# A hybrid SSM and gated-delta layer on one core: where the recurrence's buffers lie, who loads its tables, and what stands beside the last norm

## Chip, cores and metric

The kernel runs on one core of a Trainium2 chip. The metric is device time in microseconds of one launch. A core has five engines with an instruction queue each: TensorE (PE; its weight loads are shown as PEld), VectorE (DVE), ScalarE (ACT), GpSimd (POOL) and SyncE (SP), which here only issues DMAs. ACT and POOL can issue DMAs too. An engine takes its instructions in order, so one that waits holds up all behind it.

## What is computed

One layer of a decoder for 1024 prompt tokens and 8 decode rows, in float32, with model width 1024:

- `h = rms_norm(x)`, then one wide projection `h @ w_in` into z, x/B/C, dt, q/k/v, a gate, beta, a, and two merge gates.
- A Mamba-2 branch: causal convolution of width 4, silu, then a chunked scan with a state per head. `S <- S * decay + B^T (dt x)`, and `y = (masked C B^T) (dt x) + C S`; then `y = rms_norm((y + D x) * silu(z))` in four groups of 512 channels.
- A gated delta branch: convolution, silu, l2 norms of q and k, and per chunk and head the solve of a unit lower triangular system `(I + A) sol = rhs`, then the recurrence `v_new = u - w S`, `o = q_g S + (masked q k^T) v_new`, `S <- S * g + k_g^T v_new`; then `rms_norm(o) * silu(gate)`.
- `x += (sigmoid(m1) * (y @ W1) + sigmoid(m2) * (o @ W2)) @ w_out`, then a SwiGLU feed-forward of width 2816, a per-layer embedding gated by a sigmoid, and a final rms_norm.
- The last states of both branches are outputs, for the prompt and, after one step, for the 8 decode rows.

## The kernel before

**Dense work.** A wide product is made of dense tiles of 128 output channels: 8 blocks of input channels times 3 chunks of 344 tokens (1032 tokens in all). Each float32 product is three matmuls of rounded parts (`wh*h`, `wh*l`, `wl*h`, lines 159 to 178), so a dense tile is 72 matmuls. Before each tile its weights are loaded by SP into `wraw`, ACT rounds them into `wh` (L138) and DVE makes the rest `wl` (L139). Results leave PSUM by an ACT copy.

**Order.** The pieces of the program are written as one sequence, and a planner decides at build time, with a model of durations, in which order each engine gets its instructions; only a few stretches have a PE order written out by hand (`weave`, which lays dense tiles between the steps of the scan). The order is fixed at run time. A tile of a pool with a tag and `bufs` buffers takes a buffer that is free by the planner's clock; the instruction that first writes it waits on the chip until the earlier user is done with it.

**The scan.** `ssd(g)` runs the Mamba-2 scan for channel group g (four groups) over 8 chunks. Its result is written in place into four tiles `X[0..3]` (named `Xt`, 1024 columns each, pool `sa`). After the last chunk the state is transposed by PE, copied by ACT into `so` (L923) and written out (L924). `so` has the tag `sdt`, of which there is one buffer; the other users of that buffer are `u` in `ssm_dec` (L750 to 752), the first operation of the decode step, and `vbd` in the decode step of the delta branch. `ssm_dec` loads decode states into tiles of the tag `sd`, of which there are four buffers, updates them on DVE (L753) and writes them out (L754).

**The gate and the norm of a group.** `ssm_gate` multiplies `X` by silu(z) and sums squares into `sqs`; between its steps stand calls of `ssm_dec`. `ssm_norm_out(g)` makes row sums on PE, a square root and a reciprocal, sends the 1024 factors through DRAM (`rn_d`, L957) to get them on all partitions (`srb`, L959), multiplies `X` (L961) and writes it to `y_d` from ACT's queue (L962). For g = 0 to 2 it is called within the next group's convolutions. After the last group two dense tiles are left over of a list of filler tiles (`fill(FILL[4] - 2, FILL[4])`); they stand ahead of `ssm_norm_out(3)`.

**The recurrence of the delta branch.** When the scan's pools close, three pools open in their space: `gr0` (`r0`), `gr2` (`r2`) and `gr1` (`r1`), in this order. The loop at the end runs over 8 chunks with a pair of units each, `unit(0, c)` and `unit(1, c)`, four heads to a unit. A unit

1. loads `at` (256 KB) and, for each of four 32-row blocks, a piece of a table of inverted diagonal blocks into `U` (`EB<-e_d`, L1050, 16 KB) and, for three of them, its transpose into `db` (`DB<-dd_d`, L1052, 16 KB). Between them POOL zeroes the diagonal blocks of `at` (L1053). So a unit has seven table loads, all on SP, ahead of its loads of `kg`, `qg`, `qk` and `vb`;
2. multiplies `at` and `db` on PE, copies the product into `MT` (ACT, L1063), and builds the rest of the inverse in `U` in three steps of PE and DVE (L1071);
3. takes the old state off (`res`, L1080 and L1081, from the second chunk on), multiplies by `U`, copies to `vn` (L1087), makes the new state `gs`, the output `on`, its norm and its transpose, and writes it to `og_d` (L1119) from the same tile `on`.

`EB`, `DB` and `MT` are zeroed once by POOL at the start (L1032), which may only happen when what lay in their space is dead. `MT` is in `r1`; `res` shares the tag `on` (two buffers) with `on`; `gs` (four buffers) and `vn` (two) are in `r2`.

Beside the units of a chunk PE has dense tiles: the filler tiles from 15 on for chunks 0 to 3, the SSM branch product (from `y_d`) for chunks 4 to 6.

If the pools lie as they are declared, the tile sizes in the code put the scan's tiles at (KiB per partition) 0 to 12 solve tables, 12 to 41 `sw`, 41 to 49 `Bt` and `Ct`, 49 to 65 the four `Xt`; and the recurrence's before at 0 to 8 `EB`, 8 to 12 `DB`, 12 to 34 the loads, 34 to 38 `kt`, 38 to 42 `on`, 42 to 46 `vn`, 46 to 54 `gs`, 54 to 58 `MT`. So `MT` and half of `gs` lie where `Xt` was.

Of the kernel before, what the change touches and what calls it, by code (L numbers as in the profile page):

```python
# [8 lines left out]
F32 = mybir.dt.float32  # L9
# [7 lines left out]
P = 128  # L17
# [16 lines left out]
FILL = (3, 6, 9, 12, 15, 17, 20, 22, 24)  # L34
# [5 lines left out]
def hybrid_step(  # L40
# [9 lines left out]
    V, S, G, TE = nc.vector, nc.scalar, nc.gpsimd, nc.tensor  # L50
    dma = nc.sync.dma_start
# [148 lines left out]
    hacts, hs = half_slabs("h")  # L200
# [13 lines left out]
    e_d = dr.tile([8, 4, NC, 32, 32], F32, name="e_d")  # L214
    dd_d = dr.tile([8, 4, NC, 32, 32], F32, name="dd_d")
# [25 lines left out]
    with (  # L241
# [3 lines left out]
        r0 = gain_cols(p0)  # L245
# [205 lines left out]
    def fill(lo, hi):  # L451
        for _ in fill_units(lo, hi):
            pass
# [249 lines left out]
    dp = pD.enter_context(tc.tile_pool(name="dp", bufs=1, reuse_waits="tile"))  # L703
# [70 lines left out]
    with (  # L774
# [63 lines left out]
        def ssd(g, Bt, Ct, X):  # L838
# [80 lines left out]
            t = pt.tile([P, 512], F32, name="pt")  # L919
            for i in range(4):  # L920
                TE.transpose(t[:, i * P : i * P + P], st[:, i * P : i * P + P], ident)
            so = dp.tile([P, 4, P], F32, name="so", tag="sdt")
            S.copy(so.rearrange("p i n -> p (i n)"), t)  # L923
            dma(o_ssm_p[0, 0, h0 : h0 + 8].rearrange("(i a) q n -> (a q) i n", a=2), so)  # L924

# [24 lines left out]
        def ssm_norm_out(g, X, sqs):  # L950
            t = pt.tile([P, 512], F32, name="pt")
            row_sums(t, sqs)
            rr = dp.tile([P, P], F32, name="srr", tag="sdj")
            S.activation(rr, t[:, :P], AF.Sqrt, bias=b_eps, scale=1.0 / 512)
            V.reciprocal(rr, rr)
            for j in range(2):
                dma(rn_d[g, 4 * j : 4 * j + 4], rr[j::32])  # L957
            rb = s1.tile([P, NP], F32, name="srb", tag="sqs")
            dma(rb, rn_d[g].rearrange("c l -> (c l)").partition_broadcast(P))  # L959
            for i in range(4):  # L960
                V.scalar_tensor_tensor(X[i], X[i], gain(G_SSM, 4 * g + i), rb, ALU.mult, ALU.mult)  # L961
                S.dma_start(y_d[4 * g + i], X[i])  # L962

        last, side = None, solves()
        for g in range(4):
# [14 lines left out]

            weave(ssd(g, Bt, Ct, X), 17, units(), 3 * (FILL[g + 1] - FILL[g]) + 6, side)
            last = ssm_gate(g, X, zs)
        fill(FILL[4] - 2, FILL[4])
        ssm_norm_out(3, *last)
        for _ in side:
            pass
        for i in range(28, 32):
# [35 lines left out]
    with (  # L1023
# [3 lines left out]
    ):  # L1027
        EB = [r0.tile([P, 4, P], F32, name=f"EB{i}") for i in range(4)]
        DB = [r0.tile([P, 4, P], F32, name=f"DB{i}") for i in range(2)]
        MT = [r1.tile([P, 4, P], F32, name=f"MT{i}") for i in range(2)]  # L1030
        for t in EB + DB + MT:
            G.memset(t, 0.0)  # L1032
        state = [None, None]
# [4 lines left out]
        def unit(b4, c):  # L1038
            hs = slice(4 * b4, 4 * b4 + 4)
            U, db = EB[(2 * c + b4) % 4], DB[b4]  # L1040
# [6 lines left out]
            at = load(at_d, "at2")  # L1047
            for b in range(4):
                r = slice(32 * b, 32 * b + 32)
                dma(U[r, :, r], e_d[hs, b, c].rearrange("h j i -> j h i"))  # L1050
                if b < 3:
                    dma(db[r, :, r], dd_d[hs, b, c].rearrange("h j i -> j h i"))  # L1052
                G.memset(at[r, :, r], 0.0)  # L1053
            kg, qg, qk, vb = load(ktok_d, "kg"), load(qg_d, "qg2"), load(qk_d, "qk2"), load(vb_d, "vb2")
            kt = r2.tile([P, 4, C], F32, name="kt2")
# [19 lines left out]
            if c > 0:  # L1075
                ks = quad(py.tile([P, 512], F32, name="py"))
                for h in range(4):
                    mm(ks[:, h], kt[:, h], s[:, h])
                r = r2.tile([P, 4, P], F32, name="res", tag="on")
                V.tensor_tensor(r, ks, bc(fkb[:, c, hs], 2, [P, 4, P]), ALU.mult)  # L1080
                V.tensor_tensor(vb, vb, r, ALU.subtract)  # L1081
                yield 1
            vp = quad(py.tile([P, 512], F32, name="py"))
            for h in range(4):
                mm(vp[:, h], U[:, h], vb[:, h])
            vn = r2.tile([P, 4, P], F32, name="vn")
            S.copy(vn, vp)  # L1087
            yield 1
            up = quad(py.tile([P, 512], F32, name="py"))
            for h in range(4):  # L1090
                mm(up[:, h], kg[:, h], vn[:, h])
            s2 = r2.tile([P, 4, P], F32, name="gs", bufs=4)
            if c == 0:
                V.tensor_copy(s2, up)
            else:
# [675 lines left out]
```

## Time and profile before

| | |
|---|---|
| median of 3 runs | 2613.71 us (2613.59 to 2615.52) |
| the profiled execution | 2612.65 us, its span 2610.6 us, mean granted TensorE clock 0.996 |
| PE busy | 2561.8 us, 98% of the span |
| DVE, ACT, POOL busy | 1778.1, 1120.2, 264.0 us |
| DMA | 320 MB, 123 GB/s over the span |

The span runs from the first instruction to the last; 2.05 us of the execution's time lie outside it. PE is busy all but some 49 us. The scan's four groups run from about 425 to 1105 us, the last norm and the start of the recurrence lie at 1107 to 1185 us, and the recurrence ends at about 1535 us. A matmul's busy time overlaps the next one's, so rates are read from counts in a stretch, not from busy times.

### The profile page before, as it was taken

To read this page: it belongs to the slowest core of one execution; us is meant where nothing else is said; L and a number is where in the kernel's file an instruction comes from. 1 tells how busy PE (TensorE), PEld (TensorE's weight loads), DVE (VectorE), ACT (ScalarE), POOL (GpSimd) and SP (SyncE) were. 2 spreads that over 40 slices of the span, in tenths; PEclk is the share of its full clock that TensorE was granted. 3 is DMA by queue.
4 is the path that set the end of the run, shared out by engine and by line. 5 is a ranking of instruction groups with operands and counts; after the bars stand their busy time and mean duration, and the time that the engine had idled before them with its cause. 6 is when DMAs were issued, how large, how long until landed. Compare 5 with 4: busy or idle time off the path is not lost.

```text
span 2610.6 us, 46496 instructions
## 1 busy us (share of the span) xinstructions
PE 2561.8 (98%) x18155; PEld 2484.8 (95%) x18155; DVE 1778.1 (68%) x3328; ACT 1120.2 (43%) x2328; POOL 264.0 (10%) x537
## 2 busy tenths in 40 slices
PE   8999999999999999999999999999999999999998
PEld 7999999989999999889999988999999999999998
DVE  5677786698896775664455566457777777777665
ACT  5456556365373473542342235345222222223344
POOL 0221111121220210300000000012000000000110
PEclk9999999999999999999999999999999999999999
DMA  4354453444443352276664456535111111111222
GB/s 129 117 177 150 146 173 120 116 147 132 136 150 113 126 162 87 86 228 197 181 205 146 123 181 235 164 115 171 50 49 49 55 54 56 49 49 45 62 84 91
DMA packets 429913, 320.16 MB, mean 123 GB/s; under 512 B 43537, under 2 KB 392634, under 8 KB 428414
## 3 DMA queue, kind: packets, MB, share of 16 engines
q1 hardware_dynamic: 425148, 304.19, 38.6%
q10 hardware_dynamic: 2626, 8.97, 0.9%
q0 software_dynamic: 1920, 4.03, 0.4%
q8 instruction: 143, 2.34, 0.4%
q14 instruction: 76, 0.62, 0.1%
HBM read 236.64 MB, written 80.74 MB: 122 GB/s over the span
## 4 chain that ended last, share of the span: by engine, by line
PE 84%; DVE 5%; DMA 5%; ACT 3%; issue 2%; POOL 0%; SPq 0%; DVEq 0%; ACTq 0%; POOLq 0%
PE pd L69 62%; PE py L69 10%; PE pt L69 6%; PE pz L69 3%; DMA out_dram<-so 1%; DVE wl L139 1%; ACT sdt L752 1%; DMA bc<-bcd_d 1%; DVE sdj L758 1%; PE pt L856 0%; DMA eb<-eas_d 0%; DMA sg<-gate_d 0%; DVE ca L574 0%; DMA pe_d<-g 0%; DVE sd L753 0%
## 5 line engine op out<-in xcount | busy, mean ns | idle before, releaser
L69 PE MATMUL pd<-h,wh 128*128 128x344 f32 x4080 | 988.1, 324 | 2.4 <-ACT wh L138 1.7
L69 PEld LDWEIGHTS pd<-h,wh 128*128 128x128 f32 x4080 | 706.0, 189 | 10.5 <-issue 5.1
L69 PE MATMUL pd<-h,wl 128*128 128x344 f32 x2040 | 659.3, 323 | 2.4 <-DVE wl L139 2.2
L138 ACT CAST wh<-wraw 128x512 fp32r<-128x512 f32 (+1 forms) x354 | 216.7, 613 | 520.3 <-PE pd L69 357.4
L69 PEld LDWEIGHTS pd<-h,wl 128*128 128x128 f32 x2040 | 385.5, 189 | 5.3 <-DVE wl L139 4.1
L139 DVE TENSOR_TENSOR wl<-wraw,wh 128x512 fp32r<-128x512 f32 (+1 forms) x354 | 246.8, 698 | 196.0 <-ACT wh L138 190.3
L69 PE MATMUL pd<-gu,wh 128*128 128x344 f32 (+2 forms) x1056 | 248.6, 319 | 0.0
L69 PE MATMUL pd<-y,wh 128*128 128x344 f32 x768 | 187.7, 325 | 0.0
L69 PEld LDWEIGHTS pd<-gu,wh 128*128 128x128 f32 x1056 | 182.4, 188 | 0.0
L69 PE MATMUL pd<-gu,wl 128*128 128x344 f32 (+2 forms) x528 | 169.2, 320 | 0.0
L1566 DVE TENSOR_TENSOR acc<-acc,pd 128x344 f32<-128x344 f32 x216 | 109.6, 511 | 44.0 <-PE pd L69 39.8
L69 PEld LDWEIGHTS pd<-y,wh 128*128 128x128 f32 x768 | 132.7, 189 | 1.8 <-issue 0.8
L69 PE MATMUL pd<-y,wl 128*128 128x344 f32 x384 | 123.8, 322 | 0.0
L560 ACT COPY raw<-pd 128x344 f32<-128x344 f32 x144 | 62.6, 438 | 118.0 <-PE pd L69 108.9
L69 PE MATMUL pd<-bq,wh 128*128 128x258 f32 (+1 forms) x572 | 108.1, 285 | 0.0
L69 PEld LDWEIGHTS pd<-gu,wl 128*128 128x128 f32 x528 | 99.2, 188 | 0.0
L574 DVE SCALAR_TENSOR_TENSOR ca<-raw,cwm,ca 128x1056 f32<-128x1056 f32 x72 | 96.4, 1338 | 2.0
L574 DVE SCALAR_TENSOR_TENSOR ca<-raw,cwg,ca 128x1056 f32<-128x1056 f32 x72 | 95.3, 1323 | 1.5
L849 ACT ACTIVATE ab<-ab,ncolA 128x128 f32<-128x128 f32 x256 | 81.8, 391 | 33.3 <-POOL ab L845 27.2
L69 PE MATMUL pd<-o,wh 128*128 128x344 f32 x384 | 92.3, 323 | 3.0 <-DVE sgp L1351 2.2
L69 PE MATMUL pd<-h,gw 128*128 128x384 f32 (+1 forms) x576 | 94.8, 323 | 0.0
L69 PE MATMUL pd<-mx,wh 128*128 128x258 f32 x512 | 92.8, 283 | 0.0
(584 smaller groups left out, 5221.7 us busy)
## 6 DMA issues: line engine op xcount, KB each, us to landing
wraw<-in_w_in_dram SPq DMA_DIRECT2D x87, 512.0 KB
ab<-acs_d SPq DMA_DIRECT2D x32, 512.0 KB
out_dram<-sd SPq DMA_DIRECT2D x48, 256.0 KB
wraw<-in_w_ffn_in_dram SPq DMA_DIRECT2D x24, 512.0 KB
ru<-in_w_ffn_in_dram SPq DMA_DIRECT2D x22, 512.0 KB
wro<-in_w_ffn_out_dram SPq DMA_DIRECT2D x72, 128.0 KB
sg_d<-mg SPq DMA_DIRECT2D x16, 516.0 KB
bb<-rk_d SPq DMA_DIRECT2D x8, 1024.0 KB
```

The lines of the kernel that those rows point to most:

```text
L69: TE.matmul(o, l, r, start=start, stop=stop)
L138: S.copy(wh[:, :n], raw[:, k0 : k0 + n])
L139: V.tensor_tensor(wl[:, :n], raw[:, k0 : k0 + n], wh[:, :n].bitcast(F32), ALU.subtract)
L560: S.copy(raw[:, 3 + t0 : 3 + t0 + n], o[:, :n])
L574: V.scalar_tensor_tensor(ca, raw[:, j : j + CONVN], w[j], ca, ALU.mult, ALU.add)
L752: S.activation(u[:, b], bcs[0][:, b], AF.Copy, scale=xdtd[:, pair, bb : bb + 1])
L758: V.scalar_tensor_tensor(t, s[:, b], 1.0, bcs[1][:, b], ALU.mult, ALU.mult, accum_out=ydec[g][:, i % 4, bb : bb + 1])
L849: S.activation(ab[:, h], ab[:, h], AF.Exp, bias=ncolA[:, c, h0 + h : h0 + h + 1])
L1566: V.tensor_tensor(a, a, o, ALU.add)
```

## The change

```diff
@@ ssd, after the last chunk
-            so = dp.tile([P, 4, P], F32, name="so", tag="sdt")
+            so = dp.tile([P, 4, P], F32, name="so", tag="sd", bufs=4)
@@ after the last group
-        fill(FILL[4] - 2, FILL[4])
+        fill(FILL[4] - 2, FILL[4] - 1)
         ssm_norm_out(3, *last)
+        fill(FILL[4] - 1, FILL[4])
@@ the recurrence's tiles
-        MT = [r1.tile([P, 4, P], F32, name=f"MT{i}") for i in range(2)]
+        MT = [r0.tile([P, 4, P], F32, name=f"MT{i}") for i in range(2)]
+        GS = [(r0 if i < 3 else r1).tile([P, 4, P], F32, name=f"gs{i}") for i in range(4)]
@@ unit
-                dma(U[r, :, r], e_d[hs, b, c].rearrange("h j i -> j h i"))
+                G.dma_start(U[r, :, r], e_d[hs, b, c].rearrange("h j i -> j h i"))
                 if b < 3:
-                    dma(db[r, :, r], dd_d[hs, b, c].rearrange("h j i -> j h i"))
+                    G.dma_start(db[r, :, r], dd_d[hs, b, c].rearrange("h j i -> j h i"))
                 G.memset(at[r, :, r], 0.0)
@@
-                r = r2.tile([P, 4, P], F32, name="res", tag="on")
+                r = r2.tile([P, 4, P], F32, name="res", bufs=1)
@@
-            vn = r2.tile([P, 4, P], F32, name="vn")
+            vn = r0.tile([P, 4, P], F32, name="vn", bufs=2)
@@
-            s2 = r2.tile([P, 4, P], F32, name="gs", bufs=4)
+            s2 = GS[(2 * c + b4) % 4]
```

There are six edits. The scan's last state goes out through a tile of the tag `sd` instead of `sdt`. One of the two filler tiles is written behind the last norm. `MT`, `vn` and three of the four `gs` are in `r0`, the pool that lies lowest; by the same arithmetic `MT` is then at 12 to 16 KiB, the three `gs` at 16 to 22, the loads at 22 to 44 with `vn` behind them, and only `kk`, `dd`, the fourth `gs` and part of `on` are left where `Xt` was. The states `gs` are four named tiles instead of four buffers in turn. `res` has a buffer of its own. And the 112 table loads (7 for each of 16 units) are issued by POOL instead of SP.

## Rows read from the trace of the kernel before

**Rows 1.** The page's first part: each engine's busy time, share of the span and instructions.

```profile
PE 2561.8 (98%) x18155; PEld 2484.8 (95%) x18155; DVE 1778.1 (68%) x3328; ACT 1120.2 (43%) x2328; POOL 264.0 (10%) x537
```

**Rows 2.** Who PE waited for, over the whole span: who, then us in total, times, longest.

```profile
PE pt L69 <- DMA EB<-e_d: 4.1, 1, 4.1
PE pd L69 <- DVE wl L139: 3.6, 4, 1.2
PE pt L69 <- ACT MT L1063: 2.3, 1, 2.3
PE pd L69 <- ACT wh L138: 1.7, 1, 1.7
PE pt L69 <- issue: 1.3, 1, 1.3
```

**Rows 3.** PE in three stretches: from and to, length, busy us (matmuls), granted clock, DMA share, GB/s.

```profile
571.10:580.70 9.60, 6.90 (x25) 0.64 0.58 171
...
600.00:620.00 20.00, 20.00 (x128) 1.00 0.64 217
...
1143.30:1154.10 10.80, 6.71 (x26) 0.68 0.92 276
```

**Rows 4.** ACT's instructions in order of time at the end of the first scan: start, duration, engine and line; in brackets the idle time ahead and what ended it.

```profile
567.00 1.28 ACT L752 ACTIVATE sdt<-bc,xdtd 128x128 f32<-128x128 f32 x4 [3.71 <-DMA out_dram<-so]
...
572.34 0.62 ACT L138 CAST wh<-wraw 128x512 fp32r<-128x512 f32 x1
```

**Rows 5.** PE's instructions in order of time at the same place.

```profile
571.03 0.32 PE L69 MATMUL pd<-h,wl 128*128 128x344 f32 x1
573.01 0.58 PE L69 MATMUL pd<-h,wh 128*128 128x344 f32 x2 [1.66 <-ACT wh L138]
574.63 0.65 PE L69 MATMUL pd<-h,wl 128*128 128x344 f32 x1 [1.04 <-DVE wl L139]
```

**Rows 6.** SP's DMA issues around the first scan's end: the last two of four loads into `sd`, the write of `so`, the first decode state's write, and the next load into `sd`.

```profile
523.79 1.49 SPq L748 DMA_DIRECT2D sd<-in_state_ssm_dram  x2
...
562.19 0.58 SPq L924 DMA_DIRECT2D out_dram<-so  x1
568.69 0.38 SPq L754 DMA_DIRECT2D out_dram<-sd  x1
572.17 0.38 SPq L748 DMA_DIRECT2D sd<-in_state_ssm_dram  x1
```

**Rows 7.** SP's DMA issues at the recurrence's start, of the second unit of chunk 0: `at`, and the last piece of `DB`; then PE's product of the two in PE's order of time.

```profile
1128.27 1.08 SPq L1044 DMA_DIRECT2D at<-at_d  x1
...
1143.14 0.50 SPq L1052 DMA_DIRECT2D DB<-dd_d  x1
...
1147.53 1.99 PE L69 MATMUL pt<-DB,at 128*128 128x96 f32 x8 [4.09 <-DMA EB<-e_d]
```

**Rows 8.** POOL's instructions in order of time at the recurrence's start.

```profile
1136.56 0.90 POOL L1053 MEMSET at<- 32x128 f32 x4 [24.02 <-DMA at<-at_d]
...
1159.98 0.90 POOL L1053 MEMSET at<- 32x128 f32 x4 [19.44 <-DMA at<-at_d]
1160.93 1.00 POOL L1032 MEMSET MT<- 128x512 f32 x2
```

**Rows 9.** ACT's copies into `MT` for both units of chunk 0, and in the chain of work that ended last (start, us, what) the load of `at` for chunk 1.

```profile
1161.50 0.95 ACT L1063 COPY MT<-pt 128x384 f32<-128x384 f32 x2 [5.24 <-POOL MT L1032]
...
1150.83 9.04 DMA at<-at_d
```

**Rows 10.** DVE's instructions in order of time in chunk 1.

```profile
1182.55 0.69 DVE L1080 TENSOR_TENSOR res<-py,fkb 128x512 f32<-128x512 f32 x1 [2.15 <-DMA og_d<-on]
1183.16 0.21 DVE L1141 COPY qkb<-pt 128x64 f32<-128x64 f32 x1
```

**Rows 11.** Prices of DMA issues: DMAs of 16 KB that POOL issues elsewhere (ns least, median, most, then first and last start), their time to landing, the table loads on SP, and POOL's waits for `at` over the whole span.

```profile
L499 POOL DMA_DIRECT2D eas_d<-ea_d x8: 563/594/618, 83.6 to 87.3; - x8
...
DMA to landing us min/median/max: 4.2/6.6/7.5
...
L1052 SPq DMA_DIRECT2D DB<-dd_d x48: 303/437/1437, 1110.0 to 1446.5; - x48
...
POOL at L1053 <- DMA at<-at_d: 168.8, 14, 38.7
```

**Rows 12.** The last norm in order of time: its last sum of squares on DVE, its row sums on PE, the first two of its four products on DVE.

```profile
1115.91 1.22 DVE L944 TENSOR_TENSOR sqs<-sqs,zr 128x1024 f32<-128x1024 f32 x1 [0.39 <-ACT zr L943]
...
1130.66 0.64 PE L69 MATMUL pt<-sqs,oneh 128*32 128x128 f32 x16
...
1145.87 2.48 DVE L961 SCALAR_TENSOR_TENSOR Xt<-Xt,gcols,srb 128x1024 f32<-128x1024 f32 x2 [0.78 <-DMA srb<-rn_d]
```

**Rows 13.** The DMA engines in stretches of 10 us: from and to, length, granted clock, DMA share, GB/s.

```profile
1127.00:1137.00 10.00, 1.00 0.69 200
1137.00:1147.00 10.00, 1.00 0.87 254
1147.00:1157.00 10.00, 0.66 0.98 331
```

**Rows 14.** All engines in two stretches, busy us (instructions) of each, then clock, DMA share and GB/s: the rest of the recurrence, and a later stretch in which POOL's 18 instructions are DMA issues.

```profile
1200.00:1530.00 330.00, 329.87 (x2481) 317.85 (x2480) 175.51 (x368) 98.78 (x281) 14.33 (x62) 1.00 0.55 160
...
1781.00:1803.00 22.00, 22.00 (x153) 21.98 (x151) 18.35 (x30) 15.49 (x35) 9.43 (x18) 1.00 0.90 297
```

## The prediction

> **What bounds the kernel now.** First the engines' busy shares [rows 1]: PE is busy 2561.8 of 2610.6 us and no other engine above 68%, so the time can only fall where PE stands still or runs slowly. Then the list of what PE waited for [rows 2]. Most of its entries are single events, and four of them meet a line of the diff: `EB<-e_d` (4.1 us), `MT` (2.3), one wait for `wh` (1.7), and one of 1.3 for which only "issue" stands. Then PE by stretches, to see what a wait costs beyond itself [rows 3]. At an undisturbed place 128 matmuls take 20 us, 0.156 each. In 571.1 to 580.7 there are 25, which would take 3.9 us and took 9.6: 5.7 lost, though the waits there are only 1.66 and 1.04 [rows 5]. In 1143.3 to 1154.1 there are 26: 4.1 against 10.8, 6.7 lost with a wait of 4.1. The rest is the granted clock, on average 0.64 and 0.68 there: after PE had stood, it went on between full speed (2.4 GHz) and half of it. So the four places hold 5.7 + 6.7 + 2.3 + 1.3 = 16.0 us, 0.6% of the time, and that is about all that this diff can win. The rest of the recurrence has nothing to give: from 1200 to 1530 PE is busy 329.87 of 330 us [rows 14].
>
> **The change part by part.** The sum is made against the profiled execution, 2612.65 us (span 2610.6 and 2.05 around it); the median of the runs, 2613.71, is 1.06 above it.
>
> *`so` in a tile of `sd`.* ACT stood 3.71 us at the decode step's first write into `sdt`, until the write of `so` from that buffer had landed [rows 4]. Behind it in ACT's queue was the cast of the next weights, at 572.34, and PE, ready after 571.03 plus a matmul, got its weights at 573.01 and the second half at 574.63 [rows 4, 5]. Without the 3.71 the cast starts at 568.6 and ends, 0.62 later, at 569.3, some 2 us before PE asks. That removes both waits and with them the slow clock: 5.7 us. What is late next: all four buffers of `sd` were filled by 525 us, long before `so` goes out at 562.19 [rows 6], so `so` has to take one that the decode step gives back. Such a buffer's write goes out at 568.69 and its next load at 572.17, 3.5 us of landing. If ACT meets that wait at the copy into `so`, it stands up to 3.5 us again, of which 2 are covered by the slack. Bounds: between 5.7 won and 1.5 more lost than now (3.5 less the slack of 2). The planner, which knows that the buffer is taken, can lay the copy behind other work of ACT, so I take the end near the whole gain: 5.2. After the other three scans nobody on PE is late by it (there is one wait for `wh` in all [rows 2]); there I count nothing.
>
> *The tables on POOL.* PE waited 4.1 us for the tables of the second unit of chunk 0 [rows 2]. SP issued the last `DB` piece at 1143.14 [rows 7], when PE was already through with its dense tile, and 4.4 us later, at 1147.53, PE went on [rows 7]. They were late because of their place in SP's queue, behind state writes that wait for DVE. POOL is idle there from 1112.5 to 1136.6 [rows 8]. Its issues of 16 KB cost 0.56 to 0.62 us [rows 11]: 14 for both units are 8.3 us, so they are out by about 1121 and, with the 4.2 to 7.5 us of landing in the same rows, there by 1129, ahead of PE by 14 us. Wins 6.7 with the slow clock. SP loses 112 issues of 0.437, 49 us over the recurrence, on no path of its own. POOL gains 112 x 0.59 = 66 us over some 340, where it has now 14 of 330 [rows 14]. What is late next is `at` of that unit: loaded by SP at 1128.27, zeroed by POOL at 1136.56 to 1137.46 [rows 7, 8]. If the planner now lets PE come to that product before 1137.5 instead of at 1143.3, PE stands there. Bounds: 6.7 won; or nothing won if POOL's pieces stand behind that zeroing (1137.5 plus up to 6 x 0.59 plus 4.2 to 7.5 of landing ends at 1145 to 1149, about where PE went on before). Between them I take the nearer one, POOL's idle stretch, less 1.5 us: 5.2.
>
> *`MT` and `gs` off `Xt`.* ACT's copies into `MT` waited 5.24 us for POOL's zeroing [rows 9], which lay behind the zeroing of chunk 1's `at` and so behind a load of 9.04 us [rows 8, 9]. In the scan's early tiles the zeroing can run with that of `EB` and `DB`. PE's 2.3 us go, bounds 0 to 2.3; I take 2.3. The first unit's inverse can then be built before the filler tiles instead of after them.
>
> *`res` and `vn` by themselves.* At 1182.55 `res` had waited 2.15 us for the write of `og_d` out of `on`; behind it on DVE stood the copy that gives a PSUM bank back, at 1183.16 [rows 10], and PE's 1.3 us ended right after. With its own buffer `res` waits for DVE alone. Bounds 0 to 1.3; I take 1.3. One buffer for two units costs nothing, since both its uses are on DVE, in order.
>
> *One dense tile behind the last norm.* PE's work is the same: 72 matmuls, 11.3 us at 0.156. The row sums move from 1130.66 to about 1119, possible since the last sum of squares ends at 1117.1 [rows 12]; the products on DVE, now at 1145.87, come up to 11 us earlier, and with them four writes of 512 KB from ACT's queue. PE waits for none of it directly: 0. Its price is traffic: those 2 MB fall into 1136 to 1147, where the DMA engines are at 0.69 to 0.87, instead of at 0.98 [rows 13], beside the loads of the first units. Bounds: 1 us won by an earlier DVE, 2 lost by later loads; 0 taken.
>
> *Rearrangement.* Every edit moves the planner's clock, and PE takes its order from it. For waits of the size of the smaller ones in [rows 2] that turn up in new places I add 1.0 (bounds 0 and 5).
>
> Sum: 5.2 + 5.2 + 2.3 + 1.3 - 1.0 = 13.0 us. 2612.65 - 13.0 = 2599.65; with the 1.06 of the median, **2600.7 us**, 0.5% faster.
>
> A page of the Trainium skill speaks against the third of the six edits: "DMA: Bandwidth & Descriptors", section "Issuing engines are not separate DMA queues", says that DMAs of all engines run on the same 16 DMA engines and that issuing from another one saves only the time of the issuing queue. The trace agrees in part: at 1147 to 1157 the DMA engines were 98% busy [rows 13], yet the late tables were late in being issued [rows 7]. By the rule alone the 5.2 of the tables would not come, and the sum would be 2605.9.
>
> **The rivals.**
>
> *The wait moves from `sdt` to `sd`.* For it: the four full buffers and 3.5 us of landing [rows 6]. Against: the slack of 2 us. Then the 5.2 are missing: 2605.9.
>
> *The loads are the limit, not who issues them.* For it: shares of 0.87 and 0.98 [rows 13], and a single load of `at` of 9.04 us [rows 9]. PE, which now comes to the recurrence earlier, waits for `at`, `vb` and `kg` of the first units instead of for tables and `MT`, and the 5.2, 2.3 and 1.3 at the recurrence's start are taken back: 2600.7 + 8.8 = 2609.5, by part of it 2605 to 2609. This is where the rule of the Trainium skill leads. Against: `at` was there 6 us before PE in chunk 0 [rows 8].
>
> *The planner spends what it wins.* New waits of 13 us elsewhere: 2613.7, no change. Against: PE had next to none from 1200 to 1530 [rows 14].
>
> *POOL's queue is the wrong one: slower.* POOL takes its work in order and stood 168.8 us in 14 waits for `at`, up to 38.7 [rows 11]; until now nothing that PE needs soon was behind them. A table piece that stands behind such a zeroing comes after the load of `at`, up to six issues of 0.59 (3.5 us) and a landing of 4.2 to 7.5: some 9 us after `at`, where now PE can start 1 us after it. It decides from the point where `at` lands less than 9 us before PE's product with it. That holds in chunk 0 for the second unit (6 us) and in chunk 1 for both units, the first of which is zeroed at 1159.98 [rows 8], if their products move up with the rest. With three units at 9 us and the 2.6 of slow clock that went with the wait at 1147: 3 x 11.6 = 34.8 lost against 16 at stake: 2613.7 - 16.0 + 34.8 = 2632. Against: POOL's idle stretch before 1136, a later stretch where 18 issues took 9.43 us, 0.52 each, at 0.90 DMA share [rows 14], and that from chunk 2 on the tables have a chunk's length of slack.
>
> **How the numbers follow.** A change within 0.2%, 5.2 us, can't be told from none by a measurement of this kernel. Forecast, 2596 to 2604: 0.52. `sd` (2605.9): 0.13. Loads (2605 to 2609.5): 0.14, half of it beyond 2608.5. No change: 0.08. Slower: 0.13. Faster 0.52 + 0.13 + 0.07 = 0.72; same 0.07 + 0.08 = 0.15; slower 0.13. The likeliest case's own range is 2596 to 2604. The range of 8 in 10 begins at 2594, 3 us below the whole 16 us, for small waits that go by themselves, and reaches through the faster rivals and half of the no-change case, to 2613.5; it leaves out the slower rival and some 0.06 more.
>
> **What would show it.** Right: no wait of ACT for `out_dram<-so` and no wait of PE for `wh` near 573, full clock there; the `DB` issues on POOL before 1125 and no PE wait for `EB<-e_d`; POOL's zeroing of `MT` next to that of `EB`, near 1110; no wait of `res` for `og_d`; PE's row sums of the last norm near 1119. Wrong: ACT waiting for `out_dram<-sd` at L923, PE waiting for `at` or `vb` at the start, POOL's DMA issues strung out behind waits for `at`, or a mean clock below 0.996 at a new place.

## The result and the profile after

The changed kernel takes 2621.01 us in the median of 14 runs (2616.57 to 2627.9), the kernel before, run beside it, 2613.28 us: a ratio of 1.0029 with a 95% interval of 1.0020 to 1.0038. It is 0.29% slower, some 7.7 us, where 13 us were forecast as gain; the time lies 7.5 us above the upper end of the range. A repetition at the end of the study gave 1.0035 (1.0021 to 1.0049). The profiled execution took 2625.89 us, its span 2624.2; 2.9 us of that were lost to a low clock near 50 us, which the repetition's trace does not have, so places are compared from 490 us on.

The first part of the page, which answers to [rows 1]:

```profile
PE 2569.0 (98%) x18155; PEld 2490.4 (95%) x18155; DVE 1774.4 (68%) x3325; ACT 1117.8 (43%) x2329; POOL 327.1 (12%) x649
```

POOL has 112 instructions more, the table loads, and 63 us more of work; PE is busy 7 us longer for the same 18,155 matmuls. Who PE waited for, as in [rows 2] (us in total, times, longest):

```profile
PE pt L69 <- DMA DB<-dd_d: 8.5, 1, 8.5
...
PE pd L69 <- DVE wl L139: 6.6, 6, 2.4
PE pd L69 <- ACT wh L138: 3.1, 4, 1.8
...
PE pd L69 <- DVE y L189: 1.7, 1, 1.7
```

The waits for `MT` (2.3 us) and "issue" (1.3) are gone from the list. The wait for a table is still there, now 8.5 us and for `DB`, and the two for weights have grown from 5.3 to 9.7 us. Two stretches of PE show what the two large places cost (from and to, length, busy us and matmuls, granted clock, DMA share, GB/s); the first answers to the first line of [rows 3], the second to its last:

```profile
575.50:584.50 9.00, 7.23 (x34) 0.81 0.63 188
1159.00:1172.00 13.00, 4.53 (x19) 0.65 0.91 235
```

At 0.156 us each, 34 matmuls take 5.3 us: 3.7 are lost, where 5.7 were before. Of the 19 in the second stretch, 8 are the product of `DB` and `at`, 1.03 us in all at full clock elsewhere, and 11 are dense: 2.75 us of work, 10.2 lost, where 6.7 were before. In both, after PE had stood, the mean granted clock was between its two levels (0.81 and 0.65 of full speed).

**The end of the first scan**, all engines in order of time, for [rows 4 to 6]:

```profile
563.52 0.60 ACT L923 COPY so<-pt 128x512 f32<-128x512 f32 x1
...
565.68 0.58 SPq L748 DMA_DIRECT2D sd<-in_state_ssm_dram  x1
...
566.37 0.44 SPq L924 DMA_DIRECT2D out_dram<-so  x1
...
566.86 5.14 SPq L748 DMA_DIRECT2D sd<-in_state_ssm_dram  x3
...
570.70 1.14 DVE L753 SCALAR_TENSOR_TENSOR sd<-sd,dcp,sdt 128x128 f32<-128x128 f32 x4 [3.44 <-DMA sd<-in_state_ssm_dram]
...
571.88 0.99 ACT L752 ACTIVATE sdt<-bc,xdtd 128x128 f32<-128x128 f32 x3 [3.34 <-DVE sd L753]
...
575.99 0.61 ACT L138 CAST wh<-wraw 128x512 fp32r<-128x512 f32 x1
...
576.64 0.58 PE L69 MATMUL pd<-h,wh 128*128 128x344 f32 x2 [1.78 <-ACT wh L138]
```

No wait for the write of `so` is left. But the four loads of decode states, which before had gone out by 525 us [rows 6], go out at 565.68 and later, behind the copy into `so`. DVE waits 3.44 us for the first of them, ACT waits 3.34 us for DVE, and behind ACT stand the same cast of weights and the same PE wait as before. Over the whole span, ACT at L752 before (first fence) and after (second):

```profile
ACT sdt L752 <- DMA out_dram<-so: 8.5, 4, 3.7
ACT sdt L752 <- DVE sd L753: 4.2, 4, 1.6
```

```profile
ACT sdt L752 <- DVE sd L753: 15.4, 9, 3.3
```

The 8.5 us behind `so` are gone and 11.2 us behind DVE have come.

**The start of the recurrence**, POOL in order of time, for [rows 8]:

```profile
1107.97 3.15 POOL L904 TENSOR_TENSOR Xt<-Xt,eb 128x128 f32<-128x128 f32 x4 [4.91 <-DVE Xt L899]
1140.41 0.53 POOL L1132 MEMSET kqz<- 128x512 f32 x1 [29.29 <-ACT sdt L752]
1140.87 1.93 POOL L1034 MEMSET EB<- 128x512 f32 x4
1142.74 1.00 POOL L1034 MEMSET DB<- 128x512 f32 x2
1143.67 1.00 POOL L1034 MEMSET MT<- 128x512 f32 x2
1151.19 0.35 POOL L1129 MEMSET kk<- 72x128 f32 x2 [6.51 <-DVE ydec L766]
...
1151.80 0.57 POOL L1052 DMA_DIRECT2D EB<-e_d  x1
...
1159.86 0.19 POOL L1055 MEMSET at<- 32x128 f32 x1 [6.71 <-DMA at<-at_d]
1160.34 0.55 POOL L1052 DMA_DIRECT2D EB<-e_d  x1 [0.28 <-issue]
```

POOL's free stretch of before is now one wait: the zeroing of `kqz`, which needs ACT's last decode step, stands ahead of that of `EB`, `DB` and `MT`. Then a zeroing of `kk` waits for DVE, and a zeroing of `at` for a load that SP issued at 1154.12 (1107.37 before). So the first table goes out at 1151.80 and the last of the first unit at 1162.89. PE, which reached that product at 1159, went on at 1167.57. An issue costs POOL 0.55 to 0.58 us, a little less than in [rows 11].

The first copy into `MT` on ACT waits for PE alone, at 1169.66 (for POOL in [rows 9]); `res`, at 1188.20, waits for nothing (for `og_d` in [rows 10]); the last row sums on PE are at 1124.03, 12 us after the fourth copy into `so`, where [rows 12] had them 22 us after it.

### The profile page after: what moved, and what is told of

It is laid out like the page before. It is cut to its first block, busy times and chain, and to the rows that moved or that the text cites. A ratio compares the mean times of both kernels' runs of the same rounds, so it can differ in the third digit from the quotient of the medians.

```text
span 2624.2 us, 46548 instructions
## 1 busy us (share of the span) xinstructions
PE 2569.0 (98%) x18155; PEld 2490.4 (95%) x18155; DVE 1774.4 (68%) x3325; ACT 1117.8 (43%) x2329; POOL 327.1 (12%) x649
## 4 chain that ended last, share of the span: by engine, by line
PE 86%; DVE 5%; DMA 4%; ACT 2%; issue 2%; POOL 0%; SPq 0%; ACTq 0%; DVEq 0%; POOLq 0%
PE pd L69 63%; PE py L69 10%; PE pt L69 7%; PE pz L69 3%; DMA sd<-in_state_ssm_dram 1%; DVE wl L139 1%; PE pt L856 1%; DMA bc<-bcd_d 0%; DVE sd L753 0%; ACT sdt L752 0%; ACT wh L138 0%; DVE Xt L961 0%; DVE sdj L758 0%; DMA n_d<-n 0%; DMA sgp<-sg_d 0%
## 5 line engine op out<-in xcount | busy, mean ns | idle before, releaser
L1372 POOL TENSOR_TENSOR sqs<-sqs,sqt 128x1032 f32<-128x1032 f32 x6 | 15.4, 2565 | 682.1 <-ACT sqt L1371 682.1
```

The costliest lines, as they stand in the source:

```text
L1372: G.tensor_tensor(sqs[:, ts], sqs[:, ts], sq[:, :tn], ALU.add)
```

## Experiments

Each kernel was timed in turn with the kernel before on the same chip; the ratio is to that, with its 95% interval, and the last column is the median in us. (The median of before moved between 2613.3 and 2616.6 from one series to the next.)

| kernel | ratio | interval | us |
|---|---|---|---|
| the change | 1.0029 | 1.0020 to 1.0038 | 2621.0 |
| e16, the change again | 1.0035 | 1.0021 to 1.0049 | 2625.2 |
| e1, before, `kt2` and `vn` in `r0` | 0.9961 | 0.9947 to 0.9974 | 2605.4 |
| e2, the change, tables on SP | 1.0010 | 1.0001 to 1.0020 | 2619.1 |
| e3, the change, smaller `r0` | 1.0015 | 1.0007 to 1.0024 | 2620.4 |
| e4, before, tables on POOL | 1.0007 | 0.9998 to 1.0016 | 2616.8 |
| e5, before, `so` in `sd` | 0.9986 | 0.9977 to 0.9996 | 2613.3 |
| e6, before, `so` in `st` | 0.9973 | 0.9965 to 0.9982 | 2609.5 |
| e7, the change without `so` in `sd` and tables | 0.9975 | 0.9965 to 0.9985 | 2609.4 |
| e8, e1 and `so` in `st` | 0.9960 | 0.9947 to 0.9972 | 2606.1 |
| e9, the change without `so` in `sd` | 1.0015 | 1.0006 to 1.0024 | 2619.5 |
| e14, the same kernel again | 1.0012 | 1.0001 to 1.0023 | 2618.0 |
| e10, e7 and `so` in `st` | 0.9967 | 0.9956 to 0.9978 | 2606.1 |
| e11, e8 and the split of the dense tiles | 0.9956 | 0.9944 to 0.9969 | 2603.7 |
| e12, the change, zeroings off POOL | 1.0014 | 1.0001 to 1.0026 | 2619.6 |
| e13, e9, zeroings off POOL | 0.9997 | 0.9989 to 1.0006 | 2614.7 |
| e15, e13, `ydec` copies off POOL | 0.9994 | 0.9985 to 1.0003 | 2614.7 |

Where in the program the time comes or goes is read from four instructions that every kernel has: PE's first product of the first scan (at 490.1 us before), ACT's copy into `so` after the fourth scan (1108.4), its fifth and its thirteenth copy into `vn` (first units of chunks 2 and 6, at 1239.2 and 1445.6), and DVE's last addition into `acc` (2600.1). Each entry is the length of the stretch in one trace less that in the trace of before:

| us against before | scans | start of recurrence | chunks 2 to 6 | the rest |
|---|---|---|---|---|
| the change | +1.0 | +4.6 | +2.6 | +2.6 |
| e16, again | +2.2 | +6.1 | +2.8 | +4.9 |
| e2 (`so` in `sd`; SP) | +4.5 | -2.0 | +0.3 | +6.1 |
| e14 (`so` in `sdt`; POOL) | -2.8 | +2.3 | +1.9 | +4.2 |
| e7 (`so` in `sdt`; SP) | -2.1 | -2.5 | +0.1 | 0.0 |
| e13 (e14, free queue) | -1.4 | -2.8 | +1.6 | +4.8 |
| e15 (e13, `ydec` too) | -2.2 | -2.5 | +1.6 | +0.4 |
| e12 (the change, free queue) | -0.2 | +0.5 | +2.3 | +1.1 |
| e3 (the change, smaller `r0`) | +2.6 | +1.2 | +0.6 | +1.8 |
| e4 (before, POOL) | -2.3 | 0.0 | +1.6 | +1.8 |
| e1 | -1.6 | -5.2 | -1.6 | -0.4 |
| e5 | +1.9 | -1.8 | +0.1 | +1.4 |
| e6 | -0.8 | -5.0 | +0.1 | +3.9 |
| e8 (e1, `so` in `st`) | +3.2 | -6.7 | -1.5 | -0.6 |
| e10 (e7, `so` in `st`) | -1.2 | -10.3 | 0.0 | +3.0 |
| e11 (e8, split) | +2.1 | -10.5 | +0.1 | +1.5 |

The last column wanders between -0.6 and +6.1, one trace each. Most of it falls between 1500 and 1930 us, behind the last table load, and part of it is the granted clock: from 1500 to 1600 us that is 0.95 in e13 and 1.00 in e15 and in the kernel before, and e13 gets 28 matmuls fewer done there than e15, 4.4 us at 0.156. Yet e13 and e15 have the same median, so this column says nothing about the edits. Medians over many runs are what counts for totals.

**Theory A: the reach of the first pool.** In the changed kernel `r0` holds 24 tiles of 2 KB instead of 17; `Bt`, the first of the scan's long buffers, begins 20.4 tiles above the start of `r0`. e1 makes `r0` 21 tiles and changes nothing else; e3 is the change with 20.

```diff
-            kt = r2.tile([P, 4, C], F32, name="kt2")
+            kt = r0.tile([P, 4, C], F32, name="kt2", bufs=2)
-            vn = r2.tile([P, 4, P], F32, name="vn")
+            vn = r0.tile([P, 4, P], F32, name="vn", bufs=2)
```

> The kernel before, with one thing moved: kt2 and vn (two tiles of 2 KB each) are taken from the recurrence's first pool (r0) instead of r2. That pool then holds 21 tiles of 2 KB where it held 17; its storage begins at the scan's s0 buffers and reaches Bt, the first of the scan's long buffers (Bt, Ct, Xt, zt), after 20.4 tiles. Nothing of the changed kernel's own edits is in it: the tables stay on SP. Theory A (reach): the planner treats a pool as free only when the pools it lies on are done with, so the whole start of the recurrence is planned behind the last norm. Then POOL zeroes kqz ahead of EB as in the changed kernel, SP loads at after 1140 instead of 1107, PE waits 5 to 10 us near 1150 to 1170, and the time is 8 to 20 us above the kernel before: 2621 to 2633. Theory B (the tables on GpSimd are to blame): no change, 2611 to 2616. Theory C (small waits in new places are to blame): no wait near 1160, within 4 us of before.

Measured 0.9961, 10 us faster. The order came as theory A said (POOL of e1 in order of time, then PE's first product of the recurrence):

```profile
1137.45 0.53 POOL L1130 MEMSET kqz<- 128x512 f32 x1 [31.87 <-DMA out_dram<-sd]
1137.91 1.94 POOL L1032 MEMSET EB<- 128x512 f32 x4
...
1154.61 1.00 POOL L1032 MEMSET MT<- 128x512 f32 x2 [13.83 <-DMA y_d<-Xt]
```

```profile
1159.79 1.10 PE L69 MATMUL pt<-DB,at 128*128 128x96 f32 x8 [1.35 <-DMA EB<-e_d]
```

`kqz` stands ahead of `EB`, and the recurrence begins 28.6 us later than before. But the price was wrong in sign: PE waits 1.35 us for its tables where it waited 4.1, and the stretch up to chunk 2 is 5.2 us shorter. PE had its dense tiles to do first. That the planner laid them there because it knew the loads to be late is what the order suggests; no run separates it, nor the reach from the two tiles' new places.

In e3 the reach is undone (`vn` back in `r2`, two more `gs` in `r1`):

```diff
-        GS = [(r0 if i < 3 else r1).tile([P, 4, P], F32, name=f"gs{i}") for i in range(4)]
+        GS = [(r0 if i < 1 else r1).tile([P, 4, P], F32, name=f"gs{i}") for i in range(4)]
-            vn = r0.tile([P, 4, P], F32, name="vn", bufs=2)
+            vn = r2.tile([P, 4, P], F32, name="vn")
```

> The changed kernel with vn back in r2 and two of the four gs in r1 instead of r0, so that the first pool holds 20 tiles of 2 KB and ends 800 bytes short of Bt. The tables stay on GpSimd, and so, MT, res and the two-sided dense tile stay as changed. Theory A (reach): EB, DB and MT are zeroed right after the scan's last additions on POOL (near 1110), at is loaded near 1107 to 1115, the table loads go out before 1130, PE's wait of 8.5 us for DB is gone, and the time is 2598 to 2608, below both kernels. Theory B (tables on GpSimd are to blame): the tables still come late behind the waits for at, PE waits 5 us or more near 1150 and the time stays at 2616 to 2630. Theory C: 2612 to 2620, with small waits in new places.

Measured 1.0015, 2620.4 us, far above the 2598 to 2608 of theory A. The zeroing and the first tables came early, as expected of A (first fence, POOL), but PE stood at the second unit:

```profile
1111.72 1.93 POOL L1034 MEMSET EB<- 128x512 f32 x4
...
1115.47 0.57 POOL L1052 DMA_DIRECT2D EB<-e_d  x1
...
1152.74 0.92 POOL L1055 MEMSET at<- 32x128 f32 x4 [9.96 <-DMA at<-at_d]
```

```profile
1153.71 2.02 PE L69 MATMUL pt<-DB,at 128*128 128x96 f32 x8 [7.51 <-POOL at L1055]
```

Now `at` of the second unit is late: SP issued its load at 1143.87 (1128.27 before), behind eight state loads into `sd` from 1111.92 on; in the kernel before four stood in that time. By the ratios (1.0015 against 1.0029 and 1.0035) some 4 to 5 us of the loss come back without the reach, though the intervals overlap; 4 us above the kernel before remain. So theory A gives the cause of the new order, and of a part of the loss at most.

**The tables and `so`, one by one.** e2 and e9 take one of the two out of the change, e7 both, e4 and e5 put one into the kernel before. The edits are those lines of the change's diff.

> The changed kernel with its table loads back on SP; all its other edits stay. Theory A (reach): the first pool still holds 24 tiles of 2 KB and still reaches into Bt and Ct, so the start of the recurrence stays late: 2618 to 2628, no better than the changed kernel by more than 3 us. Theory B (tables on GpSimd are to blame): the loss goes and what so, MT, res win remains: 2600 to 2608. Theory C: within 4 us of the changed kernel, but with no large wait near 1160.

> The kernel before with its table loads on GpSimd and nothing else changed. Theory A (reach) with the prediction's step on the tables: the 4.1 us wait for EB<-e_d and the slow clock behind it go, 5 us won: 2606 to 2610. Theory B (the tables on GpSimd are to blame): 2620 to 2635, PE waiting for EB or DB in chunks 0 and 1. The rule that the issuing engine does not matter: 2612 to 2615.

> The kernel before with one line of the change: so takes a tile of sd, nothing else. Theory D (the ring): the buffers of a tag are given out in program order, so no state load that follows so can be issued until so has its buffer; the four state loads that the kernel before had in flight at 525 us go out only after 560, DVE waits for the load (3.4 us in the changed kernel) and ACT and PE wait behind DVE as they waited before behind the write of so. The same happens again at the ends of the next two scans, where the kernel before lost nothing. Then 0 to 6 us slower than before: 2614 to 2622. The prediction's step: 5.2 us faster, 2610. A wait of PE for wh near 575 decides.

> The changed kernel without so in sd and with the tables back on SP: MT, gs, vn, res in their new places and one dense tile on each side of the last norm. Its first pool reaches into Bt and Ct as that of the changed kernel does. Theory E (two bad edits among good ones): the late start of the recurrence that comes with the reach is a gain of 8 to 10 us, as in the kernel with kt2 and vn moved, and the two edits that are taken out cost it: 2602 to 2608. Rival (the dense tile split or the new places cost as well): 2612 to 2620.

> The changed kernel with so back in a tile of sdt; the tables stay on GpSimd. With the runs so far it is the fourth corner of a square: the other edits alone (7 us below before), with so in sd (3 above), with so and tables (8 above). If so and the tables each cost their part whatever the other does: so 10, tables 4 to 5, so 3 us below before, 2611 to 2615, and at the ends of the first three scans the trace is as in the kernel before. If the tables only hurt because so makes the loads late: as the corner without both, 2607 to 2610. If the tables are the whole cost: 2618 to 2624.

Without both, the other edits win 7 us (0.9975). With either one there is a loss: `so` makes it 1.0010, the tables 1.0012 to 1.0015, both 1.0029 to 1.0035. Each costs 9 to 10 us by itself on top of the rest, and some 5 on top of the other: they partly lose the same gain. Put into the kernel before, the tables do nothing that can be measured (1.0007), and `so` wins 3 to 4 us.

Against what was expected: e2 fell into the range of theory A, e4 above that of the rule that the issuer does not matter, by 1.8 us; e5 and e7 lie between the two ranges written for them; and e9, at 2619.5, lies in that of "the tables are the whole cost", which e2 contradicts, since with the tables on SP the loss is there too.

In e4 the prediction's step on the tables stands alone. Its table issues went out when it wanted them, the wait for `EB` is gone, and PE came to that product at 1136.52 instead of 1147.53. It then stood twice (POOL's last table issue of chunk 0, then PE):

```profile
1120.23 0.55 POOL L1050 DMA_DIRECT2D EB<-e_d  x1
...
1136.52 1.10 PE L69 MATMUL pt<-DB,at 128*128 128x96 f32 x8 [3.17 <-issue]
...
1160.73 0.44 PE L69 MATMUL pt<-EB,MT 128*32 128x32 f32 x8 [3.09 <-ACT MT L1063]
```

The start of the recurrence took as long as before (0.0 in the table).

In e5 the first scan's end shows the ring as in the changed kernel:

```profile
564.75 4.92 SPq L748 DMA_DIRECT2D sd<-in_state_ssm_dram  x3
568.36 1.14 DVE L753 SCALAR_TENSOR_TENSOR sd<-sd,dcp,sdt 128x128 f32<-128x128 f32 x4 [3.05 <-DMA sd<-in_state_ssm_dram]
...
574.30 0.58 PE L69 MATMUL pd<-h,wh 128*128 128x344 f32 x2 [1.52 <-ACT wh L138]
```

The same happens at the end of the third scan, where nothing was lost before: PE is busy 27.36 of the 30 us from 930 on, against 29.71. The two traces give it 1.9 us over the scans, the runs a gain of 3 to 4 in all, so the price of this edit by itself is not known better than that; on top of the others (e7 to e2) the scans lose 6.6 us.

**`so` without a ring that is in use.** e6, e8 and e10 give `so` a buffer of `st`:

```diff
-            so = dp.tile([P, 4, P], F32, name="so", tag="sdt")
+            so = sw.tile([P, 4, P], F32, name="so", tag="st")
```

> The kernel before with so in a tile of st, the scan's own state buffer: the scan has two, one holds the last state that so is made of, the other has been read for the last time before. So so shares a ring neither with the decode step's temporaries nor with its state loads. Theory D: no wait of ACT for out_dram<-so, the state loads stay at 525 us, no PE wait for wh near 573, and the 5.7 us of that place are won: 2607 to 2611. If the stall is not the cause of the slow stretch at 571 to 581, or the planner spends it: 2612 to 2618.

> The kernel with kt2 and vn in the first pool (2605.4 us, 10 below before) and so in a tile of st in addition. Theories D and E together: the two gains add, 10 and 3 to 5: 2599 to 2603. If the planner's rearrangement takes the gain of so: 2604 to 2608.

> All edits of the change but the two that cost: the tables stay on SP, and so takes a tile of st instead of sd. If the gain of so in st (7 us alone) adds to that of the rest (7 us): 2600 to 2605. If both win the same slack at the start of the recurrence: 2606 to 2610.

e6 is 7.2 us faster than before (0.9973). The loads into `sd` stay where they were, and no wait for `so` is left:

```profile
523.92 1.50 SPq L748 DMA_DIRECT2D sd<-in_state_ssm_dram  x2
...
585.24 0.91 PE L69 MATMUL pd<-h,wh 128*128 128x344 f32 x2 [2.47 <-ACT wh L138]
```

Even so a PE wait for weights came back, at 585; the scans gained 0.8 us only and the recurrence's start 5.0. What changed there is the place of the decode steps. Of the 32 steps of `ssm_dec`, those that ACT begins behind the four copies into `so` number 32, 24, 16 and 8 with `so` in `sdt`, 31, 23, 15 and 7 with it in `sd`, and 31, 16, 8 and 0 with it in `st`, in every trace. In `sdt` no step of a group came ahead of that group's `so`; in `st` the last group's eight are done before its scan ends. So in e6 the last step on ACT ends at 1058 us instead of 1140, `kqz`, which waits for it, is zeroed 82 us earlier (before, then e6), and SP has none of the four state loads and eight state writes that it has after 1105 in the kernel before.

```profile
1140.00 0.53 POOL L1130 MEMSET kqz<- 128x512 f32 x1 [2.54 <-issue]
```

```profile
1057.89 0.53 POOL L1130 MEMSET kqz<- 128x512 f32 x1 [3.19 <-ACT sdt L752]
```

The gains do not add up in the runs: e8 is at 0.9960, as e1 alone, and e10 at 0.9967, 2 us below e7 by the ratios, with intervals that overlap. Both hit the second alternatives that were written down for them. But the reason written down for e10, that both win the same slack at the recurrence's start, is not what their traces show: that stretch is 10.3 us shorter in e10 (2.5 in e7, 5.0 in e6) and 6.7 in e8 (5.2 in e1). What is lost lies elsewhere in these traces, in the scans for e8 and in the last column for e10; why the totals do not follow is open.

**Why the tables cost on POOL.** e12 and e13 take the zeroings that wait out of POOL's queue:

```diff
-                G.memset(at[r, :, r], 0.0)
+                V.memset(at[r, :, r], 0.0)
...
-            G.memset(t.bitcast(F32), 0.0)
+            V.memset(t.bitcast(F32), 0.0)
...
-        G.memset(kqz, 0.0)
+        V.memset(kqz, 0.0)
```

> The whole change, and the zeroing of at, of kqz and of kk and dd goes from GpSimd to VectorE, so that in the recurrence GpSimd has nothing ahead of the table loads that waits. Theory F (GpSimd's order): in the changed kernel the first tables went out at 1151.8, behind a zeroing of kqz that waited 29.3 us for ACT, one of kk that waited for DVE, and one of at that waited 6.7 us for a load. Then here the 14 pieces of chunk 0 are issued between 1116 and 1128, PE's wait of 8.5 us for DB goes, and what is left of the loss is the part of so: 2611 to 2616. Rival (the loads themselves are the limit, whoever issues them): PE waits 5 us or more for at, EB or DB near 1150 to 1170 and the time stays at 2618 to 2624.

> As the run before, with so back in a tile of sdt: all the edits that are left have no known cost then. Theory F: the 12.6 us that the tables cost on GpSimd without so in sd (2619.5 against 2609.4) come back: 2605 to 2610. Rival (the loads are the limit): 2616 to 2622.

> The changed kernel with so back in a tile of sdt, once more, for a trace: 2617 to 2622 as before. Theory F: the table issues of chunk 0 on GpSimd lie after 1145, behind kqz and at, and PE waits 5 us or more for a table near 1150 to 1170; the ends of the first three scans are as in the kernel before. Rival: no wait for tables.

With the zeroings in the way (e14, POOL, then PE):

```profile
1135.09 0.53 POOL L1132 MEMSET kqz<- 128x512 f32 x1 [30.72 <-ACT sdt L752]
...
1145.21 0.57 POOL L1052 DMA_DIRECT2D EB<-e_d  x1
```

```profile
1158.38 2.00 PE L69 MATMUL pt<-DB,at 128*128 128x96 f32 x8 [7.06 <-DMA DB<-dd_d]
```

Without them (e13):

```profile
1110.08 0.57 POOL L1052 DMA_DIRECT2D EB<-e_d  x1
...
1117.17 1.09 POOL L1052 DMA_DIRECT2D EB<-e_d  x2
```

```profile
1152.87 1.10 PE L69 MATMUL pt<-DB,at 128*128 128x96 f32 x8 [1.12 <-issue]
```

The 14 pieces of chunk 0 are out by 1118.3, as the prediction had wanted, and the wait of 7.1 us is down to 1.1. The start of the recurrence gains 5.1 us (+2.3 to -2.8) and is as good as with the tables on SP (-2.5). In the runs 0.0015 to 0.0021, 4 to 5 us, come back, with and without `so` in `sd`, though the intervals overlap. So POOL's order is the cause at this place. Both times are outside what theory F forecast, though: e12, at 2619.6, lies in the range of the rival, but without the rival's sign (PE waits 3.5 us at its first product and for no table), and is level with e2, which has the tables on SP (1.0014 and 1.0010); e13 lies between the two ranges, at 0.9997 where e7 has 0.9975: some 6 us of what the tables cost there are somewhere else.

> As the run with so in sdt and the zeroings on VectorE (2614.7), and the small copies of ydec into mg, which stood on GpSimd between the table loads of chunks 3 and 4, go to VectorE as well. Theory F, second place: between 1319 and 1382 that run lost 2.3 us against the kernel with the tables on SP, with PE waiting for y, because the copies stood behind table issues that wait for PE. Then no PE wait for y near 1325, the 2 us come back: 2610 to 2613. Rival (the second place is traffic, not order): the loss between 1319 and 1382 stays, 2613 to 2617.

```diff
-        G.tensor_copy(t[:, NP:], dec)
+        V.tensor_copy(t[:, NP:], dec)
```

Measured 0.9994, no different from e13, in the rival's range, and the loss of 1.6 us in chunks 2 to 6 stayed: here theory F fell. In the table above the kernels with the tables on POOL lose 1.6 to 2.8 us there, but for e3 (0.6), and those with SP 0.3 at most. So up to 2 of the 6 us are placed; the rest is not, and why is open. No run has the tables on POOL together with `so` in `st`, where `kqz` is done long before them.

**More of the same.** e11 has the split of the dense tiles on top of e8:

> kt2 and vn in the first pool, so in a tile of st, and one dense tile on each side of the last norm; nothing else of the change. The row sums of the last norm come 6 us earlier than with both dense tiles ahead of them. If that is worth something once the recurrence's start is planned behind the norm: 2600 to 2604. If not, as without the split: 2605 to 2608.

Its time is in the first range, but by the ratios it is at 0.9956 against 0.9960, with intervals that overlap, so a worth of the split is not shown. With 2603.7 us, e11 is the fastest kernel of the study, below both: 0.44% under the kernel before and 0.73% under the change. The last run repeated the change:

> The changed kernel once more beside the run before it, for its time on the same chip: 2617 to 2624, and a trace in which the first scan's end waits for the load into sd and the tables of the first chunk wait behind GpSimd's zeroings, as before. If the stretch near 40 us runs at full clock this time, its span is some 3 us shorter than in the first trace.

The two places are the same, and the clock at 40 to 60 us was full. The time, 2625.2 us, lies above the range, and the span is 2.3 us longer than in the first trace instead of 3 shorter; 2.3 of that are in the last column.

## Why the prediction was wrong

*`so`, 5.2 us forecast.* The step that failed is "all four buffers of `sd` were filled by 525 us, long before `so` goes out". That was true of the old program, and the new line undoes it: the buffers of a tag are given out in turn, so loads that come after `so` in the program go out after the copy into `so`. The place and the victims of the first rival ("the wait moves from `sdt` to `sd`") were right; it is DVE waiting for the load, not ACT for a buffer, and it comes at two scans' ends. Instead of 5.2 won, the scans lose 1.0 to 2.2 in the two traces of the change. Alone in the kernel before (e5) the edit won 3.7 us (1.0 to 6.0 by the interval), so some gain is there, but not by this step: the scans of e5 are 1.9 us longer. What the old stall itself is worth is not shown; e6, without it, won 7.2 us, of which the scans had 0.8.

*The tables, 5.2 forecast.* Two steps failed. "Wins 6.7 with the slow clock" failed even where its conditions were met: in e4 the pieces are out by 1120.8, and PE came to the product 11 us earlier only to stand there for 3.17 us (not for `at`, which was zeroed by 1121) and later 3.09 for `MT`; the time did not fall (1.0007). In the change itself, "POOL is idle there from 1112.5 to 1136.6" was read as room; it was room only as long as no instruction with a wait was ordered into it. The zeroing of `kqz` was, with 29.29 us. The slower rival had the mechanism (a table behind a zeroing that waits) and the price right: 11.6 us a unit were worked out and 10.2 measured in the stretch 1159 to 1172. It had the units wrong: it named three, the second of chunk 0 and both of chunk 1, and the one that was hit is the first of chunk 0, so its 2632 was too high. The forecast of issues by 1121 is what e13 shows once POOL has nothing else to wait for, with PE's wait at 1.1 us.

By the Trainium skill, "DMA: Bandwidth & Descriptors", section "Issuing engines are not separate DMA queues", another issuer saves only issue time, since all run on the same 16 DMA engines. The trace agrees: from 1100 to 1530 us the queues' share of the 16 engines was (e7, tables on SP; kind of queue, then packets, MB, share)

```profile
q1 hardware_dynamic: 128345, 70.86, 57.3%
```

and with the tables on POOL (e13)

```profile
q1 hardware_dynamic: 111658, 68.74, 54.9%
q0 software_dynamic: 3584, 1.84, 2.4%
```

57.3% both times, for nearly the same bytes in all (73.5 and 73.2 MB). The rival drawn from it, 2609.5, did not come: at the start of the recurrence the change lost by the order of issue, not by the loads. (The prediction calls the move of the table loads the third of the six edits; in the list of edits it is the last.)

*`MT` and `gs`, 2.3 forecast.* The wait is gone, and `MT` is zeroed next to `EB`, but at 1143.67 and not near 1110. What the step overlooked is the size of `r0`: it looked at what lies under each moved tile and not at how far the whole pool then reaches. The reach moves the recurrence's start back: SP issues the first load of `at` at 1107 to 1115 us in the kernels with 17 or 20 tiles and at 1139 to 1156 in those with 21 or 24. The zeroing of `EB` is late (1135 to 1141) only where that of `kqz` was put ahead of it on POOL; in e13, with 24 tiles and `kqz` on DVE, it is at 1106. A later start by itself was no loss in e1, which gained; with POOL's order it set the trap for the tables.

*`res` and `vn`, 1.3 forecast:* the wait is gone as forecast; no run has this edit or that of `MT` alone, so what they are worth is not shown. *The dense tile, 0:* right within what e11 against e8 can tell. Allowing for this run's lag of 3.9 us the row sums are within 1 us of where they were expected.

*Rearrangement, -1.0 with bounds 0 and 5.* This term was mis-sized too. One move of two tiles (e1) rearranges for 10 us of gain, and the edits of the change, which win 7 us without two of their number, lose 3 to 8 with them. The four places held 16 us in the profile of before; what an edit does to the order of everything near it is of the same size and of either sign.

## What to carry over

A prefetch in the trace belongs to the order in which a tag's buffers are given out: putting another tile into that tag puts off every later load, so look for a tag whose buffers nothing near needs; that `so` held back the decode steps from `sdt` as well showed only when it left both tags. An idle stretch of an in-order queue is free for a transfer only if nothing that waits can be ordered ahead of it; before moving DMA issues there, take the waiting instructions out or count them. When tiles are moved between pools, look at how far each pool then reaches, and measure every edit alone and together, since what they are worth did not add up here.

## What was not expected of the hardware

The same 16 KB table piece is 128 packets when SP issues it and 32 when POOL does: in the row of the software queue above, 3584 packets for 112 pieces are 32 each. Of packets under 512 bytes there are 19,832 in e7 and 5,479 in e13 in that window, a difference of 14,353, some 128 for each of the 112 pieces. The share of the DMA engines' time did not change by it (57.3%), and the landing took 3.8 and 4.1 us in the median for `EB` and `DB` from POOL, against the 6.6 of the other 16 KB DMAs in [rows 11].
